# A Strassen-Winograd encoder layer: the last product of each gate/up unit moved behind the next unit's first, four early units in step, another pace for the modulation sums, another order of tile allocation

## The chip, the cores and the metric

One core of one Trainium2 chip runs one launch of the whole layer. The metric is the device time of that launch in microseconds. The trace is of one more execution, the profiled one.

## What is computed

A bidirectional encoder layer on x of 1024 tokens by 1024 features, float32. Nine vectors of 1024 (shift, scale and gate of three blocks) come from the condition c by one large matrix-vector product, and the two feed-forward blocks are SwiGLU with D_FF = 2816:

```
mod = silu(c) @ w_ada + b_ada          # 1024 x 9216, split into nine
h = modulate(rms_norm(x, g_ffn1), sh_f1, sc_f1)
x = x + 0.5 * gt_f1 * swiglu(h, w1_gu, w1_down)
h = modulate(rms_norm(x, g_mix), sh_m, sc_m)
x = x + gt_m * (concat(rms_norm(mla(h)), rms_norm(gqa(h))) @ w_out)
h = modulate(rms_norm(x, g_ffn2), sh_f2, sc_f2)
x = x + 0.5 * gt_f2 * swiglu(h, w2_gu, w2_down)
return rms_norm(x, g_final)
```

## The kernel before

Every matrix product is made of three matmuls on operands split into a high and a low part (uh and ul, B11h and B11l and so on): `split` (lines 100 to 108) casts on ScalarE (L105) and subtracts on VectorE (L106), into a ring of 9 such pairs. The gate/up product of each feed-forward block is a Winograd form of Strassen with seven products for each unit of 128 output columns of either gate or up. There are NU = 22 units. The weights A11, A12, A22 and their sums S1 to S4 are the stationary operands; the activations B11, B21, B22 and their sums T1 to T4 are the moving ones. One product of one unit is 12 matmuls of 128x512 (`prod`, L485 to L487).

For the first NE = 8 units, A11 B11 and A12 B21 are done ahead, while the T operands are still being built (`early`, `early2`, and for units 4 to 7 `early_rest`, lines 550 to 566). `run` (lines 611 to 652) then does the rest unit by unit: S2 T2, S1 T1, S3 T3, (A12 B21,) S4 B22, A22 T4. S3 T3 and A22 T4 accumulate into the same bank c. VectorE reads c after S3 T3 (`post`, L501 or L507), and only then may A22 T4 write it again. After each product `tick` (lines 200 to 205) makes two splits for units to come, and every second tick pumps one step of the stream `ada`.

That stream carries the modulation vectors that are not needed at once: seven blocks of 1024 (numbers 2, 4, 3, 5, 7, 6, 8), eight tiles each of 128x1024 (512 KB) of w_ada. For each block `ada_use` (lines 304 to 316) clears one accumulator tile acc on GpSimd (L310), loads the bias row into it (L311), and then adds each tile, times a column of silu(c), on VectorE (L313). After the eighth, TensorE sums acc over the partitions: for a gate with two matmuls by a matrix of ones (`mod_gate`, L342), for a shift or scale with eight matmuls of one column (`mod_cols`, L328). There is one acc tile, so the next block's L310 waits for those matmuls, and there are two tiles for loads (tag "ada"). What is left of the stream is done after the units, before the down projection begins:

```
    ffn.run()
    while ada.i < len(ada.specs):
        ada.pump(1)
    bg.finish()
```

The down projection (`down`) then multiplies the g tiles, written to HBM by `g_out` and loaded back, with the down weights (L729 to L731), whose quarters are summed on VectorE (L698) as they come. A scheduler sets the final order of the instructions on each engine; it may hoist an instruction whose buffers are free, and each engine runs its own list in order. SyncE issues most of the loads, in order, too.

Of the kernel before, what the change touches and what calls it, by code (L numbers as in the profile page):

```python
# [35 lines left out]
NQ0 = 4  # L36
NE = 8
# [146 lines left out]
def encoder_layer(ctx: ExitStack, tc: tile.TileContext, a: dict, out: bass.AP):  # L184
# [11 lines left out]
    st = Stream(nc, rawp, ring)  # L196
    st.raw_pools["graw"] = (lambda: t2("graw"), 2)
    bg = Background()

    def tick(n=2):  # L200
        bg.step()
        st.pump(n)
        ada_ticks[0] += 1
        if ada_ticks[0] % 2 == 0:
            ada.pump(1)


# [6 lines left out]
    def t2(name, dt=F32):  # L214
        return tmp.tile([P, 512], dt, tag="t2", name=name, bufs=6)

    def small(n, name):
        return sm.tile([P, 16], F32, tag="small", name=name, bufs=20)[:, 0:n]
# [55 lines left out]
    def use_banks(kinds):  # L274
        banks.update(kinds=kinds, n=0, pair=None)

    def ps2():
        return p2p.tile([P, 1024], F32, tag="ps2", name="ps2")

    def ps1():  # L280

        if banks["pair"] is not None:
            p = banks["pair"][:, 512:1024]
            banks["pair"] = None
            return p
        kind = banks["kinds"][banks["n"] % len(banks["kinds"])]
        banks["n"] += 1
        if kind[0] == "2":
            p = ps2()
            if kind == "2":  # L290
                banks["pair"] = p
            return p[:, 0:512]
        return (p0p if kind == "0" else p1p).tile([P, 512], F32, tag="ps1", name="ps1")
# [5 lines left out]

    ada = Stream(nc, None, None)  # L300
    ada.hold = ada.hold_step = 0
    ada_ticks = [0]

    def ada_use(blk, kt):
        def use(raw):
# [140 lines left out]
    class GateUp:  # L446
# [2 lines left out]
            self.c1, self.s, self.bank, self.g = {}, {}, {}, {}  # L449

        def alloc(self, pool, names):
            for k2 in range(2):
                for nm in names:
                    h = pool.tile([P, 2, 512], F32R, name=f"{nm}h{k2}")
                    l = pool.tile([P, 2, 512], F32R, name=f"{nm}l{k2}")
                    for e in range(2):
                        self.Bh[nm, 2 * k2 + e] = h[:, e, :]
                        self.Bl[nm, 2 * k2 + e] = l[:, e, :]
# [91 lines left out]
        def early_rest(self, builds):  # L550

            K4 = (0, 1, 2, 3)
            for u in range(NQ0, NE):
                self.bank[u] = ps1()
                self.prod(self.bank[u], u, "A11", "B11", K4, True, True)
                self.store_p1(u)
                next(builds, None)
                st.pump(2)
                bg.step()
                self.prod(self.bank[u], u, "A12", "B21", K4, False, True)  # L560
                self.early_out(u)
                next(builds, None)
                st.pump(2)
                bg.step()
            for _ in builds:
                pass

# [23 lines left out]
        def early2(self, prepare):  # L591

            K4 = (0, 1, 2, 3)
            for u in range(NQ0):
                self.bank[u] = ps1()
                self.prod(self.bank[u], u, "A11", "B11", K4, True, True)
                self.store_p1(u)
# [6 lines left out]
            for u in range(NQ0):  # L604
                self.prod(self.bank[u], u, "A12", "B21", K4, False, True)
                self.early_out(u)
# [4 lines left out]
        def run(self):  # L611
            use_banks(SIX)
            K4 = (0, 1, 2, 3)
            self.load_p1(0)
            for u in range(NU):
                early = u < NE
                self.load_p1(u + 1)
                if early and u % 2:
                    self.g["A21"] = gtp["g"]()
                    nc.sync.dma_start(self.g["A21"], ge_d[u // 2])  # L620
                if not early:
                    self.bank[u] = ps1()
                    self.prod(self.bank[u], u, "A11", "B11", K4, True, True)
                    self.keep_p1(u)
                    tick()
                c1 = self.c1.pop(u)
                b = ps1()
                self.prod(b, u, "S2", "T2", K4, True, True)
                u2 = t2("U2")
                nc.vector.tensor_tensor(u2, b, c1, op=ALU.add)  # L630
                tick()
                e = ps1()
                self.prod(e, u, "S1", "T1", K4, True, True)
                u4 = t2("U4")
                nc.vector.tensor_tensor(u4, e, u2, op=ALU.add)
                tick()
                c = ps1()
                self.prod(c, u, "S3", "T3", K4, True, True)
                self.post(u, 1, 1, c, u4)
                tick()  # L640
                if not early:
                    self.prod(self.bank[u], u, "A12", "B21", K4, False, True)
                    self.post(u, 0, 0, self.bank[u])
                    tick()
                d = ps1()
                self.prod(d, u, "S4", "B22", K4, True, True)
                self.post(u, 0, 1, d, u4)
                tick()
                self.prod(c, u, "A22", "T4", K4, False, True)
                self.post(u, 1, 0, c, u2)  # L650
                del self.bank[u]
                tick()

    def gu_specs(i):
        for u in range(NU):
# [755 lines left out]
    for s in range(NQ + LAG + 3):  # L1411
        if s < NQ:
            i, t = divmod(s, NT)
            p = scores(i, t)
            nm = small(1, "nm")
# [303 lines left out]
```

## Time and profile before

| | us |
|---|---|
| median of 3 runs | 2065.8 (2059.12 to 2625.26) |
| the profiled execution, its own time | 2058.35 |
| its span, first to last instruction | 2056.6 |
| first gate/up, early units included, in the span | 23.8 to 508.7 |
| second gate/up, early units included, in the span | 1392.3 to 1830.4 |

TensorE's granted clock was 0.984 of full speed over the span. A stretch of the trace is told by the microseconds from the start of the span. In a timeline an idle time before an instruction stands in brackets with what ended it.

### The profile page before, as it was taken

What the parts mean: (1) busy time and instruction counts of PE and PEld (TensorE: products, weight loads), DVE (VectorE), ACT (ScalarE), POOL (GpSimd) and SP (SyncE); (2) the same over time, 40 slices, a digit from 0 to 9 for tenths busy, and PEclk for the clock granted to TensorE, in tenths of its full rate; (3) what the DMA queues carried; (4) which work ended last, traced back from release to release, by engine and by line L of the source; (5) the groups of instructions that cost most, each with busy time, mean ns of one, the idle gap of its engine ahead of it and who ended that gap; (6) DMA issues with size and microseconds to landing.
All of it is one profiled execution on the core that took longest, in us unless ns stands there. A gap on an engine that the chain in (4) does not pass through costs nothing. (4 is left out here: it accounts for less than half of the span.)

```text
span 2056.6 us, 28024 instructions
## 1 busy us (share of the span) xinstructions
PE 1974.8 (96%) x10301; PEld 1678.4 (82%) x10301; DVE 1570.0 (76%) x2381; ACT 973.6 (47%) x1865; POOL 473.5 (23%) x428
## 2 busy tenths in 40 slices
PE   5889999999999999899999999998999999999998
PEld 4667888887788888788889998996788888877886
DVE  7998888974697777788798877677886666647976
ACT  6522322232344652677787777466323333324444
POOL 1643434332000023111210000005443332310011
PEclk8899999999999999999999999999999999999999
DMA  8276655544843343623253330343443332358223
GB/s 343 102 241 215 205 173 192 188 140 153 306 162 107 137 134 108 179 73 108 88 169 78 83 82 32 142 136 128 150 174 113 118 109 81 124 184 337 98 93 118
DMA packets 90550, 303.30 MB, mean 147 GB/s; under 512 B 9848, under 2 KB 22427, under 8 KB 76588
## 3 DMA queue, kind: packets, MB, share of 16 engines
q1 hardware_dynamic: 81018, 274.21, 39.5%
q0 software_dynamic: 7040, 23.07, 2.9%
q10 hardware_dynamic: 2354, 4.22, 0.5%
q8 instruction: 81, 1.33, 0.3%
q14 instruction: 57, 0.47, 0.1%
HBM read 220.98 MB, written 80.49 MB: 147 GB/s over the span
## 5 line engine op out<-in xcount | busy, mean ns | idle before, releaser
L105 ACT CAST uh<-raw 128x512 fp32r<-128x512 f32 (+1 forms) x343 | 210.3, 622 | 213.7 <-PE ps L486 134.5
L106 DVE TENSOR_TENSOR ul<-raw,uh 128x512 fp32r<-128x512 f32 (+1 forms) x343 | 255.0, 749 | 42.6 <-ACT uh L105 42.3
L105 ACT CAST uh<-S 128x512 fp32r<-128x512 f32 x198 | 121.9, 621 | 329.4 <-PE ps L486 247.4
L729 PE MATMUL ps<-uh 128*128 128x512 f32 x616 | 240.9, 393 | 5.8 <-ACT uh L105 5.8
L730 PE MATMUL ps<-ul,uh 128*128 128x512 f32 x616 | 241.5, 392 | 1.4 <-DVE ul L106 1.4
L731 PE MATMUL ps<-uh,ul 128*128 128x512 f32 x616 | 240.9, 391 | 0.0
L106 DVE TENSOR_TENSOR ul<-S,uh 128x512 fp32r<-128x512 f32 x198 | 193.7, 982 | 46.0 <-ACT uh L105 42.9
L1416 DVE TENSOR_REDUCE nm<-ps 128x1 f32<-128x1024 f32 x128 | 155.5, 1215 | 70.5 <-PE ps L223 40.8
L426 POOL TENSOR_TENSOR S<-raw 128x512 f32<-128x512 f32 x88 | 126.3, 1443 | 257.8 <-DVE ul L106 132.6
L521 POOL TENSOR_TENSOR g<-g 128x512 f32<-128x512 f32 x88 | 124.8, 1418 | 227.2 <-DVE g L508 226.3
L1434 ACT CAST ph<-ps 128x512 fp32r<-128x512 f32 x256 | 138.1, 590 | 80.0 <-PE ps L1433 79.7
L1444 DVE TENSOR_TENSOR pl<-ps,ph 128x512 fp32r<-128x512 f32 x256 | 163.9, 682 | 0.0
L1439 ACT ACTIVATE pe<-ps,nm 128x1024 f32<-128x1024 f32 x128 | 143.7, 1123 | 16.7 <-DVE nm L1416 16.5
L729 PEld LDWEIGHTS ps<-uh 128*128 128x128 f32 x616 | 116.2, 189 | 31.4 <-ACT uh L105 7.5
L730 PEld LDWEIGHTS ps<-ul,uh 128*128 128x128 f32 x616 | 116.4, 189 | 27.8 <-DVE ul L106 3.9
L731 PEld LDWEIGHTS ps<-uh,ul 128*128 128x128 f32 x616 | 116.3, 189 | 24.2
L1433 PE MATMUL ps<-ident,pe 128*128 128x128 f32 x1024 | 134.9, 273 | 0.8 <-DVE pl L1444 0.4
L1433 PEld LDWEIGHTS ps<-ident,pe 128*128 128x128 f32 x1024 | 119.7, 141 | 19.0 <-DVE pl L1444 0.6
L105 ACT CAST uh<-hT 128x512 fp32r<-128x512 f32 x96 | 59.7, 622 | 157.1 <-PE ps L730 113.5
L1382 PE MATMUL po<-ph,V 128*128 128x256 f32 x512 | 129.7, 291 | 0.0
L1383 PE MATMUL po<-pl,V 128*128 128x256 f32 x512 | 125.8, 283 | 0.0
L233 POOL TENSOR_TENSOR r<-v,neghalf 128x1 f32<-128x1 f32 x32 | 25.5, 797 | 363.9 <-DVE v L229 363.9
(280 smaller groups left out, 5180.2 us busy)
## 6 DMA issues: line engine op xcount, KB each, us to landing
raw<-in_w_gu_dram SPq DMA_DIRECT2D x52, 1024.0 KB, 4.9
ada<-in_w_ada_dram SPq DMA_DIRECT2D x56, 512.0 KB, 3.7
g_S<-g POOLq DMA_DIRECT2D x88, 256.0 KB, 2.4
g_A<-g SPq DMA_DIRECT2D x66, 256.0 KB, 3.0
hT<-in_w_down_dram SPq DMA_DIRECT2D x16, 1024.0 KB, 8.6
raw<-g_S SPq DMA_DIRECT2D x16, 1024.0 KB, 4.9
raw<-g_A SPq DMA_DIRECT2D x12, 1024.0 KB, 4.8
x<-in_x_dram SPq DMA_DIRECT2D x16, 512.0 KB, 7.3
```

What stands on the lines that cost most here:

```text
L105: nc.scalar.copy(hi[:, 0:n], ap)
L106: nc.vector.tensor_tensor(lo[:, 0:n], ap, f32(hi[:, 0:n]), op=ALU.subtract)
L426: eng.tensor_tensor(tmps[nm], get(x), get(y), op=op)
L729: nc.tensor.matmul(p, gh[:, tsl], wh, start=start, stop=False, skip_group_check=True)
L730: nc.tensor.matmul(p, gh[:, tsl], wl, start=False, stop=False, skip_group_check=True)
L731: nc.tensor.matmul(p, gl[:, tsl], wh, start=False, stop=stop, skip_group_check=True)
L1382: nc.tensor.matmul(po[:, 0:256], V, gr.ph[:, k, :], start=(k == 0), stop=False)
L1416: nc.vector.tensor_reduce(nm, p, axis=AX.X, op=ALU.max, negate=True)
L1433: nc.tensor.transpose(out=pt[:, k, :], in_=pe[:, (4 * n + k) * P:(4 * n + k + 1) * P], identity=ident)
L1434: nc.scalar.copy(gr.ph[:, 4 * n:4 * n + 4, es], pt)
L1439: nc.scalar.activation(pe, p, AF.Exp, bias=nm, accum_out=ls[:, s % 2:s % 2 + 1])
L1444: nc.vector.tensor_tensor(gr.pl[:, nsl, es], pts[n], f32(gr.ph[:, nsl, es]), op=ALU.subtract)
```

## The change

Four edits. In `run`, the last product of a unit (A22 T4) and its post go into a function that is called after the next unit's S2 T2; the last unit's is called after the loop. In `early_rest`, units 4 to 7 do all four A11 B11 products and then all four A12 B21 products. In `alloc`, the loop over names is outside, so that both tiles of B11 come first. In `tick`, the stream `ada` is pumped by a rate in eighths; the rate is a list that holds 0, and no other line of the file writes it, so the condition `0 > 0` is never true and the 56 steps are all reached by the loop after `run`.

```
-        if ada_ticks[0] % 2 == 0:
+        if ada_ticks[0] * ada_rate[0] // 8 > (ada_ticks[0] - 1) * ada_rate[0] // 8:
             ada.pump(1)
...
-    ada_ticks = [0]
+    ada_ticks, ada_rate = [0], [0]
...
-            for k2 in range(2):
-                for nm in names:
+            for nm in names:
+                for k2 in range(2):
...
-            for u in range(NQ0, NE):
+            for u0 in range(NQ0, NE, 4):
+                us = range(u0, u0 + 4)
+                for u in us:
                     self.bank[u] = ps1()
                     self.prod(self.bank[u], u, "A11", "B11", K4, True, True)
                     self.store_p1(u)
...
+                for u in us:
                     self.prod(self.bank[u], u, "A12", "B21", K4, False, True)
                     self.early_out(u)
...
                 nc.vector.tensor_tensor(u2, b, c1, op=ALU.add)
                 tick()
+                if tail:
+                    tail.pop()()
                 e = ps1()
...
-                self.prod(c, u, "A22", "T4", K4, False, True)
-                self.post(u, 1, 0, c, u2)
-                del self.bank[u]
-                tick()
+                def last(u=u, c=c, u2=u2):
+                    self.prod(c, u, "A22", "T4", K4, False, True)
+                    self.post(u, 1, 0, c, u2)
+                    del self.bank[u]
+                    tick()
+                tail.append(last)
+            tail.pop()()
```

The order on TensorE before, where the first gate/up ends (T4 is the last unit's last product) and the down projection begins (its first row is L729):

```order
L485 MATMUL ps_4063<-T4h_576,uh 128x512
L486 MATMUL ps_4063<-T4l_577,uh 128x512
L487 MATMUL ps_4063<-T4h_576,ul 128x512
L729 MATMUL ps_4176<-uh 128x512
L729 MATMUL ps_4177<-uh 128x512
L729 MATMUL ps_4179<-uh 128x512
```

The same place on TensorE in the change (L328 and L342 are the matmuls of the modulation vectors, L740 the first of the down projection):

```order
L487 MATMUL ps_3804<-T4h_576,ul 128x512
L342 MATMUL ps_3908<-acc,ones 128x512
L342 MATMUL ps_3913<-acc,ones 128x512
L328 MATMUL ps_3945<-ones,acc 128x1 x8
L328 MATMUL ps_3982<-ones,acc 128x1 x8
L342 MATMUL ps_4019<-acc,ones 128x512
L342 MATMUL ps_4024<-acc,ones 128x512
L328 MATMUL ps_4056<-ones,acc 128x1 x8
L328 MATMUL ps_4093<-ones,acc 128x1 x8
L342 MATMUL ps_4126<-acc,ones 128x512
L342 MATMUL ps_4131<-acc,ones 128x512
L740 MATMUL ps_4176<-uh 128x512
```

All seven blocks' matmuls, which stood between the units before, now stand in a row ahead of the first down product.

VectorE in the change from the last post of gate/up (the first row) on; the list goes on with the rest of the 48 sums, and the next split for down stands behind the last of them:

```order
L507 TENSOR_TENSOR g<-ps_3804,U_3772 128x512
L106 TENSOR_TENSOR ul<-hT,uh 128x512
L508 TENSOR_TENSOR g<-g,s 128x512
L106 TENSOR_TENSOR ul<-raw,uh 128x512
L106 TENSOR_TENSOR ul<-hT,uh 128x512
L106 TENSOR_TENSOR ul<-raw,uh 128x512
L106 TENSOR_TENSOR ul<-hT,uh 128x512
L106 TENSOR_TENSOR ul<-raw,uh 128x512
L106 TENSOR_TENSOR ul<-hT,uh 128x512
L106 TENSOR_TENSOR ul<-raw,uh 128x512
L313 SCALAR_TENSOR_TENSOR acc<-ada,cact,acc 128x1024 x8
L333 SCALAR_TENSOR_TENSOR modA_111<-ps_3945,cols 128x8
```

The first block's eight sums stay early in gate/up, because its acc and its loads find free buffers; the other 48 moved to the end, and 11 of the sums of L698 (L709 in the change) stand among them.

TensorE before, in the third unit of the first gate/up, from S4 B22 to A22 T4:

```order
L487 MATMUL ps_1210<-B22h_568,ul 128x512
L485 MATMUL ps_1210<-B22h_568,uh 128x512
L486 MATMUL ps_1210<-B22l_569,uh 128x512
L487 MATMUL ps_1210<-B22h_568,ul 128x512
L485 MATMUL ps_1188<-T4h_566,uh 128x512
L486 MATMUL ps_1188<-T4l_567,uh 128x512
```

The same place in the change:

```order
L487 MATMUL ps_1185<-B22h_560,ul 128x512
L485 MATMUL ps_1213<-T2h_566,uh 128x512
L486 MATMUL ps_1213<-T2l_567,uh 128x512
L487 MATMUL ps_1213<-T2h_566,ul 128x512
L485 MATMUL ps_1213<-T2h_566,uh 128x512
L486 MATMUL ps_1213<-T2l_567,uh 128x512
L487 MATMUL ps_1213<-T2h_566,ul 128x512
L485 MATMUL ps_1213<-T2h_568,uh 128x512
L486 MATMUL ps_1213<-T2l_569,uh 128x512
L487 MATMUL ps_1213<-T2h_568,ul 128x512
L485 MATMUL ps_1213<-T2h_568,uh 128x512
L486 MATMUL ps_1213<-T2l_569,uh 128x512
```

One whole product of the next unit now stands between S4 B22 and A22 T4 (12 matmuls, of which the last is not shown).

## Rows read from the trace of the kernel before

**Rows 1.** The page, part 1: busy us, share, instructions of each engine.

```profile
PE 1974.8 (96%) x10301; PEld 1678.4 (82%) x10301; DVE 1570.0 (76%) x2381; ACT 973.6 (47%) x1865; POOL 473.5 (23%) x428
```

**Rows 2.** Stretches: us, busy (count) by engine, PE clock, DMA share, GB/s.

```profile
110.00:200.00 90.00, 79.83 (x332) 63.55 (x331) 82.68 (x93) 23.59 (x39) 34.16 (x29) 0.96 0.67 226
300.00:400.00 100.00, 99.75 (x453) 82.11 (x452) 84.94 (x101) 28.47 (x50) 36.39 (x34) 1.00 0.56 187
1400.00:1500.00 100.00, 88.16 (x382) 71.20 (x381) 79.99 (x87) 46.93 (x90) 52.09 (x36) 0.97 0.39 138
1500.00:1600.00 100.00, 100.00 (x443) 82.80 (x442) 72.29 (x94) 30.06 (x49) 39.87 (x36) 1.00 0.39 137
```

**Rows 3.** PE's waits, 0 to 110 us: total, times, longest.

```profile
PE ps L485 <- POOL acc L310: 3.5, 1, 3.5
```

**Rows 4.** PE's waits, 110 to 200 us.

```profile
PE ps L485 <- DVE s L501: 9.4, 3, 5.0
```

**Rows 5.** Timeline of PE, 140 to 155 us: start, duration, operation [idle before].

```profile
148.06 0.76 PE L485 MATMUL ps<-T4h,uh 128*128 128x512 f32 x1 [5.00 <-DVE s L501]
...
154.24 0.39 PE L485 MATMUL ps<-T2h,uh 128*128 128x512 f32 x1
```

**Rows 6.** PE's waits, 1380 to 1500 us.

```profile
PE ps L485 <- ACT c L493: 9.3, 2, 7.6
```

**Rows 7.** Tile acc: count, duration ns min/median/max, first and last start.

```profile
L328 PE MATMUL ps<-ones,acc x64: 164/250/250, 211.2 to 397.0; 128*128 128x1 f32 x64
L313 DVE SCALAR_TENSOR_TENSOR acc<-ada,cact,acc x56: 1269/1280/5112, 113.8 to 425.9; 128x1024 f32<-128x1024 f32 x56
...
L342 PE MATMUL ps<-acc,ones x12: 591/592/593, 161.7 to 442.8; 128*128 128x512 f32 x12
L310 POOL MEMSET acc<- x7: 947/955/976, 96.1 to 402.5; 128x1024 f32 x7
```

**Rows 8.** Timeline of PE: matmuls of modulation vectors, three places.

```profile
18.91 1.87 PE L910 MATMUL modp<-ones,acc 128*128 128x1 f32 x8 [1.77 <-DVE acc L783]
...
161.75 1.88 PE L342 MATMUL ps<-acc,ones 128*128 128x512 f32 x4
163.06 0.79 PE L485 MATMUL ps<-B22h,uh 128*128 128x512 f32 x1
...
211.20 1.84 PE L328 MATMUL ps<-ones,acc 128*128 128x1 f32 x16
```

**Rows 9.** Timelines, SyncE's queue and VectorE, 402 to 428 us: last block.

```profile
403.53 0.25 SPq L311 DMA_DIRECT2D acc<-in_b_ada_dram  x1
406.41 0.33 SPq L95 DMA_DIRECT2D ada<-in_w_ada_dram  x1
...
405.09 1.29 DVE L313 SCALAR_TENSOR_TENSOR acc<-ada,cact,acc 128x1024 f32<-128x1024 f32 x1 [0.73 <-issue]
...
410.06 1.29 DVE L313 SCALAR_TENSOR_TENSOR acc<-ada,cact,acc 128x1024 f32<-128x1024 f32 x1
...
425.87 1.28 DVE L313 SCALAR_TENSOR_TENSOR acc<-ada,cact,acc 128x1024 f32<-128x1024 f32 x1
```

**Rows 10.** The page, part 6: DMA issues, KB each, us to landing.

```profile
raw<-in_w_gu_dram SPq DMA_DIRECT2D x52, 1024.0 KB, 4.9
ada<-in_w_ada_dram SPq DMA_DIRECT2D x56, 512.0 KB, 3.7
```

**Rows 11.** Timelines of PE and of DVE where gate/up 1 ends.

```profile
509.04 1.20 PE L729 MATMUL ps<-uh 128*128 128x512 f32 x4 [0.30 <-ACT uh L105]
...
508.83 0.69 DVE L507 TENSOR_TENSOR g<-ps,U 128x512 f32<-128x512 f32 x1 [1.30 <-PE ps L487]
...
517.57 0.68 DVE L106 TENSOR_TENSOR ul<-raw,uh 128x512 fp32r<-128x512 f32 x1
```

**Rows 12.** Line 698: the sums of weight quarters for down.

```profile
L698 DVE TENSOR_TENSOR hT<-hT x48: 679/685/692, 564.9 to 1937.9; 128x512 f32<-128x512 f32 x48
```

**Rows 13.** PE's waits, 200 to 560 us.

```profile
PE ps L729 <- ACT uh L105: 2.2, 2, 1.9
```

More of the change, by code (lines that the diff above doesn't have):

```diff
@@ L552, in early_rest @@
             K4 = (0, 1, 2, 3)
-            for u in range(NQ0, NE):
[L554 to L564, printed above, removed]
+            for u0 in range(NQ0, NE, 4):
+                us = range(u0, u0 + 4)
+                for u in us:
+                    self.bank[u] = ps1()
+                    self.prod(self.bank[u], u, "A11", "B11", K4, True, True)
+                    self.store_p1(u)
+                    next(builds, None)
+                    st.pump(2)
+                    bg.step()
+                for u in us:
+                    self.prod(self.bank[u], u, "A12", "B21", K4, False, True)
+                    self.early_out(u)
+                    next(builds, None)
+                    st.pump(2)
+                    bg.step()
             for _ in builds:
@@ L613, in run @@
             K4 = (0, 1, 2, 3)
+            tail = []
             self.load_p1(0)
```

## Prediction

> **What bounds the kernel now.** I read the page first: TensorE is busy 96% of the span, VectorE 76% [rows 1]. Then the stretches of 50 to 100 us. In the middle of both gate/up phases TensorE has no gap (99.75 and 100.00 of 100 us) and starts 443 matmuls in 100 us, 0.226 us each, so one product of 12 takes 2.71 us there. Two stretches have gaps: 110 to 200 us, with 79.83 of 90 us busy at a clock of 0.96, and 1400 to 1500 us, with 88.16 [rows 2]. The list of waits names them: in the first TensorE waits 9.4 us in three places for L501, VectorE's read of bank c ahead of A22 T4 [rows 4]; in the second 9.3 us for L493, ScalarE's copy of an early unit's bank [rows 6]. The modulation sums cost TensorE nothing but their own few matmuls, since VectorE does them beside the products. So the change can win only in those two stretches, and it can lose wherever TensorE is made to wait.
>
> **The part that decides: the sums.** The rate holds 0 and nothing sets it, so no tick pumps the stream. The order shows the result: 8 sums stay early, 48 stand behind the last post of gate/up 1, and all the matmuls of the seven vectors stand on TensorE ahead of the first down product. TensorE cannot pass them, and the splits for down that are made before them fill the ring of 9 pairs. So the whole chain of sums is idle time of TensorE. I count it from 508.83 us, where VectorE's last post starts and the last product has ended [rows 11].
>
> Start: before the first of the 48 sums VectorE has the post and eight splits. The same eight splits took until 517.57 + 0.68 us in the trace [rows 11], 9.4 us after 508.83. The matmuls of the block that was summed early, L310 and the bias row lie beside this.
>
> One block of eight sums: the first two tiles are loaded already, each later tile needs a free one of two buffers. A sum takes 1.28 us [rows 7]. In the trace a load is issued 0.03 us after the sum that frees its buffer (405.09 + 1.29, then 406.41), and the sum that uses it starts 3.65 us later, at 410.06 [rows 9]; the page has 3.7 us [rows 10]. So two tiles take 1.28 + 0.03 + 3.7 = 5.01 us, and a block takes three such rounds and two sums: 15.0 + 2.6 = 17.6 us. Six blocks: 105.6 us. VectorE alone would need 6 x 8 x 1.28 = 61.4 us; the two buffers make the rest.
>
> Between two blocks: TensorE sums acc, GpSimd clears it (0.955 us) [rows 7], the bias row is loaded (1.56 us from the issue at 403.53 to the sum at 405.09) [rows 9], with some 0.15 us of signals. TensorE will have idled, and after idle time it runs at the lower of its clocks, 1.2 GHz: behind the wait of 5.00 us the 15 matmul starts up to 154.24 us took 6.2 us for 3.4 [rows 5], and 8 one-column matmuls at the start of the kernel took 1.87 us where 16 took 1.84 us in the busy stretch [rows 8]. So a shift or scale takes 3.7 us and a gate 2.6 us (twice the 1.31 us from 161.75 to 163.06) [rows 8]. Four transitions behind shifts and scales: 4 x 6.4 = 25.6 us; one behind a gate, with its copy and two stores in SyncE's queue ahead of the bias: 5.7 us; the last gate's matmuls: 2.6 us.
>
> The 11 sums of weight quarters that stand among them take 0.685 us each [rows 12], 7.5 us if none fell into the waits for loads; 4 us is my value, about half. Loads of down weights pass in the same queue between the pairs; at 1.2 us for each further 512 KB (4.9 less 3.7) [rows 10] a round of 5 us has room for one of 1 MB and the pair, so I add nothing.
>
> Sum: 9.4 + 105.6 + 25.6 + 5.7 + 2.6 + 4 = 152.9 us, less 0.2 us from 508.83 to 509.04 that stood there before: **+152.7 us**. Behind it down starts at the lower clock: 6.2 less 3.4 [rows 5], **+2.8 us**.
>
> The bounds: if the loads were ready always, a block would be 10.2 us and the stall 108. If each block took as long as the last one in the trace, 425.87 + 1.28 less 405.09 = 22.1 us, with other work and loads between [rows 9], it would be 180.
>
> The Trainium skill's page "DMA: Bandwidth & Descriptors", section "Anatomy of one DMA", puts the fixed part of a transfer at about 2.0 us. The trace's two sizes give 3.7 less 1.2 = 2.5 us. An estimate by the page: loads of 3.2 us, 18 rounds each 0.5 us shorter, a total 9 us lower than mine. The rows decide here, since they are these very loads.
>
> **What comes back in the first gate/up.** The matmuls of the vectors leave a TensorE that has no gaps: 64 rows at L328 are four vectors at 1.84 us, 12 at L342 three gates at 1.31 us [rows 7, 8]: **-11.3 us**. They are in the chain above. The moved A22 T4 gives VectorE 2.71 us more to read bank c. Of the waits of 9.4 us the one of 5.00 keeps 2.3 and the other two, 4.4 us together, go almost whole; with no sums on VectorE after the first block and a shorter slow stretch behind I take **-10 us**, between 0 (VectorE is just as late at the next bank) and -13 (all waits and the 2.8 us of slow clock). What is queued behind the moved product: the next unit's S1 T1, which needs nothing from it. The order on TensorE had started the next S2 T2 early here and there already, so nothing new must be ready.
>
> **Early units in step, and the allocation.** In the first feed-forward block the longest wait of the early part, 3.5 us, is for room for the T tiles, not for an early unit [rows 3]; the scheduler had interleaved the units in the old loop already. I take 0, with 3.5 us to either side. In the second, TensorE waits 7.6 us of the 9.3 for one copy [rows 6], and the copy keeps its place on ScalarE behind the casts of the T operands. TensorE has six more matmuls to do first (1.4 us), and the second wait, 9.3 less 7.6 = 1.7 us, is covered by whole products: **-3 us**, between 0 and -9.3. The order of names in the allocation moves no instruction; nothing. In the second gate/up proper there is no wait to win [rows 2].
>
> **At the start of down** TensorE waited 2.2 us for casts whose data came late [rows 13]. With 150 us to load it this is gone: **-2 us**.
>
> **Total:** 152.7 + 2.8 - 11.3 - 10 - 3 - 2 = +129 us on the profiled execution's 2058.35 us: 2187.6, so **2188 us**. That execution stands 7 us under the median of 2065.8 and 1 us under the lowest of the three; I keep its scale. A measurement tells about 2% from no change, some 41 us; three times that is forecast.
>
> **The rivals.**
> Loads hidden: if the pairs of loads kept ahead of VectorE, six blocks would be 7.4 us shorter each: 2188 - 44 = 2144 us. For it: only that the queue has room. Against it: two buffers, and the load is longer than two sums. 4%.
> Loads in each other's way: every block as long as the last one of the trace, 22.1 us: 2188 + 27 = 2215 us. For it: the down weights load through the same queue meanwhile. Against it: half the blocks run after these are in, and VectorE has no other work. 8%.
> Nothing comes back in the waits: without the -10, -3 and -2 it is 2203 us. For it: VectorE is 82.68 of 90 us busy from 110 to 200 us [rows 2], where the 8 early sums stay. 5%.
> Not slower: down's products run while the sums go on, because TensorE is fed from the ring and the vectors are needed much later. Then the stall is nothing, the slow clock too, the matmuls are only moved, and 2058 - 10 - 3 = 2045 us is left. It decides from the point at which TensorE idles under some 26 us at the end of gate/up, what the other terms give back. Against it: the rows on TensorE ahead of L740. 3%.
>
> **How the numbers follow.** My case has 80%. Its ends: fast clock in the transitions (-9), sums of quarters hidden (-4), loads shorter by the estimate's 9 us or waits that all go (-10), about 2155 us; blocks longer by 4 us, nearly the second rival's, 2212 us. The range 2152 to 2212 us takes in the third rival and leaves the first and most of the second outside. Slower by over 2%: 0.96; within 2%: 0.03; faster: 0.01.
>
> **What would show it.** After: TensorE idle but for the vectors' matmuls for about 150 us from some 490 us on, the clock low there; six groups of eight sums at L313, each 17 to 18 us long, in pairs 5 us apart; 6 us between groups, with L310 released by TensorE; the waits for L501 from 110 to 200 us under 5 us. Wrong would be: sums closer than 2 us throughout, down matmuls between the vectors', gaps of 10 us between blocks, or a gate/up phase that ends later than before.

## The result, and the profile after

The changed kernel takes 2194.6 us (median of 4 runs, 2193.35 to 2197.02); before it was 2062.9 us (median of 4). The ratio is 1.0646, with a 95% interval of 1.0621 to 1.0672; one run before, of 2625.26 us, is left out of it as slow. The forecast was 2188 us within 2152 to 2212. The profiled execution took 2194.53 us, with a span of 2192.8 us, 136.2 us longer than that of the profiled execution before.

The page of the changed kernel, TensorE's and its clock's rows of part 2 behind that of part 1, which answers to [rows 1]; in part 2 each digit is a slice of 54.8 us:

```profile
PE 1976.8 (90%) x10301; PEld 1683.7 (77%) x10301; DVE 1532.5 (70%) x2381; ACT 975.9 (45%) x1865; POOL 465.5 (21%) x428
...
PE   6889999981129999999999999999799999999998
...
PEclk7999999995559999999999999999999999999999
```

TensorE is busy as long as before (1976.8 for 1974.8 us) in a longer span. The missing time is one hole of three slices, and in them the clock stands near the lower of its two levels. The list of TensorE's waits says who made the hole. First the stretch from 470 to 720 us, then 110 to 480 us, to be held against [rows 4], and the two longest from 1500 to 1650 us, against [rows 6] (total, times, longest):

```profile
PE ps L328 <- DVE acc L313: 97.5, 4, 30.4
PE ps L342 <- DVE acc L313: 45.7, 2, 23.7
```

```profile
PE ps L485 <- DVE s L501: 5.0, 2, 4.1
PE ps L485 <- DVE g L507: 2.3, 1, 2.3
```

```profile
PE ps L485 <- ACT c L493: 8.3, 2, 6.2
PE ps L485 <- ACT es L502: 3.0, 1, 3.0
```

Six waits, one for each block that was left, cost 143.2 us (97.5 + 45.7). TensorE's timeline through the hole (start, duration, operation, idle before):

```profile
485.70 1.88 PE L342 MATMUL ps<-acc,ones 128*128 128x512 f32 x4
518.01 3.58 PE L328 MATMUL ps<-ones,acc 128*128 128x1 f32 x16 [30.43 <-DVE acc L313]
545.78 3.57 PE L328 MATMUL ps<-ones,acc 128*128 128x1 f32 x16 [24.20 <-DVE acc L313]
573.02 3.78 PE L342 MATMUL ps<-acc,ones 128*128 128x512 f32 x4 [23.66 <-DVE acc L313]
...
648.72 3.62 PE L342 MATMUL ps<-acc,ones 128*128 128x512 f32 x4 [22.01 <-DVE acc L313]
651.49 1.09 PE L740 MATMUL ps<-uh 128*128 128x512 f32 x1
```

The first vector was summed early and costs nothing. The other six stand in a row ahead of L740, the first down matmul, as the order had shown. VectorE's last post starts at 485.96 us, so the stall, counted as in the forecast from there to the first down matmul, is 651.49 - 485.96 = 165.5 us. VectorE's timeline shows what fills it, first in the first of the six blocks, then in the fifth:

```profile
485.96 0.69 DVE L507 TENSOR_TENSOR g<-ps,U 128x512 f32<-128x512 f32 x1 [1.30 <-PE ps L487]
...
495.21 2.59 DVE L313 SCALAR_TENSOR_TENSOR acc<-ada,cact,acc 128x1024 f32<-128x1024 f32 x2
500.52 1.28 DVE L313 SCALAR_TENSOR_TENSOR acc<-ada,cact,acc 128x1024 f32<-128x1024 f32 x1 [2.72 <-DMA ada<-in_w_ada_dram]
...
507.23 1.28 DVE L313 SCALAR_TENSOR_TENSOR acc<-ada,cact,acc 128x1024 f32<-128x1024 f32 x1 [2.85 <-DMA ada<-in_w_ada_dram]
...
513.57 1.28 DVE L313 SCALAR_TENSOR_TENSOR acc<-ada,cact,acc 128x1024 f32<-128x1024 f32 x1 [2.64 <-DMA ada<-in_w_ada_dram]
516.67 1.28 DVE L313 SCALAR_TENSOR_TENSOR acc<-ada,cact,acc 128x1024 f32<-128x1024 f32 x1 [1.82 <-DMA ada<-in_w_ada_dram]
...
604.09 2.60 DVE L313 SCALAR_TENSOR_TENSOR acc<-ada,cact,acc 128x1024 f32<-128x1024 f32 x2 [2.46 <-DMA acc<-in_b_ada_dram]
609.02 1.28 DVE L313 SCALAR_TENSOR_TENSOR acc<-ada,cact,acc 128x1024 f32<-128x1024 f32 x1 [2.33 <-DMA ada<-in_w_ada_dram]
611.38 1.28 DVE L313 SCALAR_TENSOR_TENSOR acc<-ada,cact,acc 128x1024 f32<-128x1024 f32 x1 [1.08 <-DMA ada<-in_w_ada_dram]
613.99 1.28 DVE L313 SCALAR_TENSOR_TENSOR acc<-ada,cact,acc 128x1024 f32<-128x1024 f32 x1 [1.32 <-DMA ada<-in_w_ada_dram]
...
618.98 1.29 DVE L313 SCALAR_TENSOR_TENSOR acc<-ada,cact,acc 128x1024 f32<-128x1024 f32 x1 [1.26 <-DMA ada<-in_w_ada_dram]
621.78 1.28 DVE L313 SCALAR_TENSOR_TENSOR acc<-ada,cact,acc 128x1024 f32<-128x1024 f32 x1 [1.52 <-DMA ada<-in_w_ada_dram]
```

In these two blocks only the first pair finds its tiles loaded; each later sum is released by a load. In the fifth block the pairs start 4.93, 4.97 and 4.99 us apart, in the first 5.31, 6.71 and 6.34. SyncE's queue in the first block shows what differs (x2 are the two loads of a pair):

```profile
496.51 1.65 SPq L95 DMA_DIRECT2D ada<-in_w_ada_dram  x2
498.20 0.43 SPq L86 DMA_DIRECT2D hT<-in_w_down_dram  x1
501.84 2.90 SPq L95 DMA_DIRECT2D ada<-in_w_ada_dram  x2
504.79 0.42 SPq L86 DMA_DIRECT2D hT<-in_w_down_dram  x1
```

Behind each of these pairs stands a load of down weights, of 1 MB (behind the third pair of the block it is one of 0.75 MB, behind the last none). In the fifth block the queue has eight loads of ada from 605.40 us on and nothing between them. The page's part 6 has the median time from issue to landing, to be held against [rows 10]:

```profile
ada<-in_w_ada_dram SPq DMA_DIRECT2D x56, 512.0 KB, 4.5
```

And four stretches: the middle of gate/up (against [rows 2]), the hole, and in it the first and the fifth block (length, then busy time and count of PE, PEld, DVE, ACT, POOL, then clock, DMA share, GB/s):

```profile
300.00:400.00 100.00, 100.00 (x442) 82.80 (x442) 58.49 (x84) 32.64 (x54) 35.52 (x33) 1.00 0.29 100
490.00:650.00 160.00, 19.29 (x70) 15.91 (x71) 74.05 (x68) 2.07 (x4) 9.19 (x11) 0.52 0.67 220
495.00:518.00 23.00, 0.00 (x0) 0.00 (x0) 10.47 (x9) 0.00 (x0) 0.56 (x1) 0.50 0.89 330
604.00:623.00 19.00, 0.00 (x0) 0.00 (x0) 10.21 (x8) 0.00 (x0) 0.00 (x0) 0.50 0.65 190
```

In the hole no engine is busy half of the time, and the DMA engines are so 0.67 of it. That mean hides two stages: in the first block, with the down weights behind the pairs, the DMA engines are busy 0.89 of the time and move 330 GB/s; in the fifth, where the sums' loads are alone, 0.65 and 190 GB/s, and there the latency of the loads sets the pace. In the middle of gate/up TensorE was full before and is full now, with a third of VectorE's work gone (58.49 for 84.94 us). What was taken off VectorE there had not kept TensorE waiting.

### The profile page after: what moved, and what is told of

The parts are those of the page before. It is cut to its first block, busy times and chain, and to the rows that moved or that the text cites. A ratio compares the mean times of both kernels' runs of the same rounds, so it can differ in the third digit from the quotient of the medians.

```text
span 2192.8 us, 28026 instructions
## 1 busy us (share of the span) xinstructions
PE 1976.8 (90%) x10301; PEld 1683.7 (77%) x10301; DVE 1532.5 (70%) x2381; ACT 975.9 (45%) x1865; POOL 465.5 (21%) x428
## 5 line engine op out<-in xcount | busy, mean ns | idle before, releaser
L740 PE MATMUL ps<-uh 128*128 128x512 f32 x616 | 240.5, 391 | 2.8 <-ACT uh L105 2.8
L106 DVE TENSOR_TENSOR ul<-S,uh 128x512 fp32r<-128x512 f32 x198 | 158.0, 803 | 55.3 <-ACT uh L105 55.3
L1445 ACT CAST ph<-ps 128x512 fp32r<-128x512 f32 x256 | 138.1, 590 | 79.7 <-PE ps L1444 79.6
L426 POOL TENSOR_TENSOR S<-raw 128x512 f32<-128x512 f32 x88 | 118.8, 1360 | 203.1 <-DMA raw<-in_w_gu_dram 99.3
L740 PEld LDWEIGHTS ps<-uh 128*128 128x128 f32 x616 | 115.7, 188 | 28.0 <-ACT uh L105 3.6
L313 DVE SCALAR_TENSOR_TENSOR acc<-ada,cact,acc 128x1024 f32<-128x1024 f32 x56 | 74.3, 1328 | 66.3 <-DMA ada<-in_w_ada_dram 52.1
```

What stands on the lines that cost most here:

```text
L106: nc.vector.tensor_tensor(lo[:, 0:n], ap, f32(hi[:, 0:n]), op=ALU.subtract)
L740: nc.tensor.matmul(p, gh[:, tsl], wh, start=start, stop=False, skip_group_check=True)
L1445: nc.scalar.copy(gr.ph[:, 4 * n:4 * n + 4, es], pt)
```

## The experiments

Three questions were open: whether the rate alone makes the whole loss, what paces a block, and what the other three edits are worth.

**Which edit costs.** The kernel before, with nothing changed but that no tick pumps the stream:

```
-        if ada_ticks[0] % 2 == 0:
+        if ada_ticks[0] < 0:
             ada.pump(1)
```

> The kernel before, with the stream of modulation sums pumped at no tick, and nothing else changed. Theory A, the pace of the sums alone makes the loss: 48 sums stand behind gate/up 1 as in the changed kernel, the stall is 160 to 170 us, and since the product A22 T4 is not moved the waits for L501 are at most a few us more: 2190 to 2206 us. Rival B, a good part of the loss comes from the three other edits (the moved product, the units in step, the allocation): under 2180 us.

Measured: 2196.8 us, ratio 1.0675 (1.0648 to 1.0701). TensorE's waits from 110 to 720 us in it:

```profile
PE ps L328 <- DVE acc L313: 97.5, 4, 29.1
PE ps L342 <- DVE acc L313: 44.1, 2, 23.0
PE ps L485 <- DVE s L501: 7.0, 2, 5.5
```

The same six waits, and a time 2 us above the changed kernel's: the rate makes the whole loss, with none of the other edits there. The opposite try is the changed kernel at the old pace, four eighths, from the start:

```
-    ada_ticks, ada_rate = [0], [0]
+    ada_ticks, ada_rate = [0], [4]
```

> The changed kernel with the rate at 4 eighths from the start, which is the pace of the kernel before: the three other edits alone. Theory A: the stall is gone, and the three edits are worth 0 to 12 us, nearly all of it from the waits for L501 between 110 and 200 us: 2048 to 2060 us. Rival B: they cost time by themselves, over 2070 us.

Measured: 2052.2 us, ratio 0.9965 (0.9951 to 0.9979). The hole is gone, and what is left beats the kernel before, by about 7 us.

**The sums from the ninth unit on**: the changed kernel with a rate of six eighths set when the units that are not early begin.

```
             for u in range(NU):
                 early = u < NE
+                if u == NE:
+                    ada_rate[0] = 6
```

> The changed kernel with one line more: the rate is set to 6 eighths at the ninth unit of gate/up 1. Theory A: all 56 sums but the first eight run beside the late units, where VectorE was 66 to 85 of 100 us busy; no stall, and the early units are free of them: 2040 to 2056 us. Rival C, 48 sums in 14 units crowd VectorE (48 x 1.28 = 61 us in some 230): TensorE waits for splits or for bank reads there, 2062 to 2090 us.

Measured: 2058.0 us, ratio 0.9994 (0.9983 to 1.0004): no gain over the kernel before, and 6 us behind the old pace. TensorE's waits from 110 to 520 us, first with the sums from the ninth unit on, then with the old pace:

```profile
PE ps L485 <- DVE s L501: 4.9, 2, 4.1
PE ps L328 <- DVE acc L313: 2.4, 1, 2.4
PE ps L485 <- DVE g L507: 2.3, 1, 2.3
PE ps L328 <- ACT c L493: 1.3, 1, 1.3
```

```profile
PE ps L485 <- DVE s L501: 4.6, 2, 4.0
PE ps L485 <- DVE g L507: 3.3, 2, 1.6
PE ps L485 <- ACT s L502: 2.0, 1, 2.0
```

The waits for the posts are 7.2 us with the stream held back beside the first units and 9.9 with it. Against these 2.7 us stand two waits of 3.7 us in all at the vectors' matmuls, where the old pace has none; in the 60 us around each (280 to 340 and 380 to 440 us) the clock is 0.97, where it is 1.00 at the old pace. Over these 120 us that is 3.6 us, and with the 1.0 us of waits it comes near to the whole difference from the first T2 product to the first down matmul (406.7 us, and 401.8 at the old pace). So the closer pace gives back more than the late start wins. The time lies between the bands of the two theories: a gain from the late start is not there, and the closer pace costs less than was feared.

**What paces a block.** Three kernels do all seven blocks after the first gate/up, from a pool of their own that opens when gate/up's tiles are gone. The first has six tiles for loads, the second the same and two accumulators, the third two tiles for loads:

```
...
+    es_ = ExitStack()
+    ep = es_.enter_context(tc.tile_pool(name="ep", bufs=1))
+    t4pool["p"] = (ep, 1)
+    ada.raw_pools["raw"] = (lambda: ep.tile([P, D], F32, tag="ada", name="ada", bufs=6), 6)
...
+    while ada.i < len(ada.specs):
+        ada.pump(1)
```

Six tiles:

> The changed kernel with the loads of the sums in a pool of six tiles in place of two, which has room only after gate/up: all seven blocks then stand behind it. Theory A, the two buffers pace the chain: a block of eight sums takes 10.3 to 12 us in place of 18 to 23, the stall is 9 + 7 x 11 + 6 x 6.4 + 3 = 127 us with one block more, and the time 2150 to 2165 us. Rival D, the queue's bandwidth, shared with the down weights, paces it: blocks stay at 18 us or more, the stall is 175 us or more with one block more, and the time 2200 us or more.

Measured: 2171.3 us (one execution). VectorE's first two blocks:

```profile
501.62 10.53 DVE L313 SCALAR_TENSOR_TENSOR acc<-ada,cact,acc 128x1024 f32<-128x1024 f32 x8 [13.81 <-DMA acc<-in_b_ada_dram]
518.56 10.53 DVE L313 SCALAR_TENSOR_TENSOR acc<-ada,cact,acc 128x1024 f32<-128x1024 f32 x8 [6.41 <-DMA acc<-in_b_ada_dram]
```

Eight sums without a gap, 10.53 us, are VectorE's own time (8 x 1.28 = 10.2), so the rival, a queue whose bandwidth holds the blocks at 18 us, falls. The time is 6 us above what was expected: the first sum starts 23.1 us behind the last post, where 9 had been reckoned. SyncE issues the first loads of ada only at 491.42 us, the bias row behind them, and the first sum waits for that row.

Two accumulators (`t4pool["p"] = (ep, 2)`):

> All seven blocks behind gate/up 1 with six tiles for loads, as in the earlier run, and two accumulators in place of one. Theory A, between blocks VectorE waits 6 us for TensorE's matmuls, the clearing and the bias row because there is one accumulator: these six gaps go nearly whole, and the time is 2135 to 2148 us against 2171. Rival, the loads (56 of 512 KB) hold the pace once the gaps are gone: gaps of 3 us or more between the groups, 2150 to 2165 us.

Measured: 2145.7 us (one execution), 25.6 us less. VectorE's first blocks in it:

```profile
498.15 9.21 DVE L313 SCALAR_TENSOR_TENSOR acc<-ada,cact,acc 128x1024 f32<-128x1024 f32 x7 [13.85 <-DMA acc<-in_b_ada_dram]
508.14 8.96 DVE L313 SCALAR_TENSOR_TENSOR acc<-ada,cact,acc 128x1024 f32<-128x1024 f32 x7 [0.78 <-DMA ada<-in_w_ada_dram]
```

The first block's eighth sum waits 0.78 us for its load, and the second block's first six follow it with no gap. So the 6.4 us between these two blocks came from the single accumulator. But the six gaps did not go nearly whole, as was expected: three later groups still waited 5 to 6 us, bias rows among the causes. From the first sum to the end of the last VectorE is idle 26 us, where with one accumulator the six transitions made 38: 12 us are saved, and that is all that the second accumulator shows. Of the other 13 us, 3.5 lie in the earlier start (498.15 for 501.62 us) and between 6 and 7 in the 11 sums of weight quarters, which stand among the blocks with one accumulator and behind them with two; the rest lies behind the stall. That the time fell into the band of the first theory was luck. Even so this stands 86 us above the kernel before.

Two tiles in the same place (`bufs=2`):

> The counterpart of the run with six tiles for loads: all seven blocks behind gate/up 1, in a pool of their own that has room only then, but with two tiles. Theory A, the two buffers make a block 18 us or more: 7 blocks x (19.5 less 10.5) = 63 us over the run with six tiles, 2225 to 2245 us. Rival, the late start or the shared queue made the difference between the runs so far: within 25 us of the run with six tiles.

Measured: 2218.8 us (one execution), 6 us below the expected band and 47.5 above six tiles. The start of its first block on VectorE:

```profile
494.81 2.60 DVE L313 SCALAR_TENSOR_TENSOR acc<-ada,cact,acc 128x1024 f32<-128x1024 f32 x2 [8.13 <-DMA ada<-in_w_ada_dram]
501.05 1.28 DVE L313 SCALAR_TENSOR_TENSOR acc<-ada,cact,acc 128x1024 f32<-128x1024 f32 x1 [3.63 <-DMA ada<-in_w_ada_dram]
```

The seven blocks took 21.1, 20.0, 18.6, 18.7, 18.6, 20.1 and 18.6 us, 135.6 in all, where six tiles took 79.7. The number of tiles alone makes 8 us in each block, and 56 us in seven; most of the way from there to 47.5 is the earlier start of the first sum (494.81 for 501.62 us). The rival, that the late start or the shared queue made the difference, falls.

**Who stands in the way of the loads.** The changed kernel, with the down weights' quarters issued from ScalarE's queue in place of SyncE's:

```
-                    self.nc.sync.dma_start(src[0](), src[1])
+                    self.nc.scalar.dma_start(src[0](), src[1])
```

> The changed kernel with the loads of the down weights' quarters issued by ScalarE's queue, where they stand in a row early in the stall and no longer between the pairs of loads for the sums. Theory A, a load of 1 MB ahead of a pair makes the first three blocks longer (22.7, 21.4 and 20.8 us against 18.3, 19.0 and 19.4 for the others): the first block takes 23 to 32 us, the second and third 18 to 19.5 us and what their weight sums add, under 2 us; the stall is 155 to 166 us, the time 2184 to 2196 us. Rival, the first blocks are long for another reason: the second and third stay at 20.5 to 21.5 us, and the time stays at 2194 us or rises.

Measured: 2202.7 us, ratio 1.0692 (1.0674 to 1.0710). VectorE's timeline, the first block and the start of the second:

```profile
496.76 3.71 DVE L313 SCALAR_TENSOR_TENSOR acc<-ada,cact,acc 128x1024 f32<-128x1024 f32 x2 [2.75 <-DMA acc<-in_b_ada_dram]
507.87 1.28 DVE L313 SCALAR_TENSOR_TENSOR acc<-ada,cact,acc 128x1024 f32<-128x1024 f32 x1 [7.40 <-DMA ada<-in_w_ada_dram]
...
517.43 1.28 DVE L313 SCALAR_TENSOR_TENSOR acc<-ada,cact,acc 128x1024 f32<-128x1024 f32 x1 [5.05 <-DMA ada<-in_w_ada_dram]
...
525.54 1.28 DVE L313 SCALAR_TENSOR_TENSOR acc<-ada,cact,acc 128x1024 f32<-128x1024 f32 x1
...
533.59 2.60 DVE L313 SCALAR_TENSOR_TENSOR acc<-ada,cact,acc 128x1024 f32<-128x1024 f32 x2
```

Now the down weights come together: from 495 to 527 us the DMA engines are busy 0.96 of the time and move 382 GB/s. The first block takes 30.1 us, and the second and third, 21.4 and 20.8 us in the changed kernel, take 18.5 and 19.05, as long as the blocks behind them (18.8 to 19.0). So it is the down weights' traffic that makes the early blocks longer, and another queue for it changes only which block pays: 124.4 us for the six, where it was 121.7. The mechanism was foreseen and the time was not: it came out above the band. The stall in the trace is 169.8 us (655.91 - 486.14), 4.3 us longer than in the changed kernel; the rest of the 8 us is not explained. The Trainium skill's page "DMA: Bandwidth & Descriptors", section "Issuing engines are not separate DMA queues", says that transfers of all issuing engines run on the same 16 DMA engines and interleave, so that spreading them saves only issue time; the rounds of 11.1 and 9.6 us in the first block agree.

**What the other edits are worth**, each at the old pace. The moved A22 T4 alone; then with the units in step but the old allocation; then with the allocation but the old early loop. The hunks are those of the diff ahead of the prediction, taken singly into the kernel before (for the first: `tail` and `last` in `run`; for the second `us = range(u0, u0 + 4)` in `early_rest` too; for the third `for nm in names` outside in `alloc`), and `[0], [4]` for the rate.

> The kernel before with the moved product A22 T4 alone, at the old pace of the sums. Theory A, read from the run with all three edits (10 us less between the first T2 product and down 1, 3 us less in gate/up 2, but 2 and 4 us more in the two early parts): the moved product brings 13 to 15 us and the units in step take back 6, so this alone is the fastest, 2043 to 2049 us. Rival: the early parts' loss belongs to the moved product or is noise, 2050 to 2056 us.

> The moved product and the units in step, with the old order of allocation, at the old pace. Theory A, the allocation moves nothing: 2050 to 2055 us, as with all three. Rival, the allocation makes the loss in the early parts: 2043 to 2049 us.

> The moved product and the new order of allocation, with the old loop over the early units, at the old pace. Theory A, the units in step make the loss in the early parts: 2043 to 2049 us, the early part before the second block's first T2 product 51 to 52 us. Rival, the allocation makes it: 2050 to 2056 us and 55 to 56 us.

| at the old pace | us | ratio, 95% | start to start of the second early part | from there to the second down |
|---|---|---|---|---|
| moved product alone | 2053.7 | 0.9957 to 0.9985 | 51.7 | 386.8 |
| moved product and step | 2053.6 | 0.9956 to 0.9983 | 55.6 | 383.7 |
| moved product and allocation | 2051.5 | 0.9944 to 0.9971 | 51.7 | 387.0 |
| all three | 2052.2 | 0.9951 to 0.9979 | 55.7 | 383.5 |

(The last two columns are of one trace each: from the first B11 product of the second feed-forward block to its first T2 product, and from there to its first down matmul. Before they were 51.7 and 386.7 us.) The four can't be told apart by their intervals. The moved product makes the whole gain, 6 to 8 us, less than the 13 to 15 us that I had expected of it; the step and the allocation are worth nothing that shows. The times of the first and the third run ended in the bands of their rivals: the step moves 4 us from one part of the trace to the other, as the table shows, but takes no time from the whole.

## Why the prediction was right, and where it was off

The forecast rested on one step, that the rate of 0 puts 48 sums and their matmuls ahead of the first down matmul and that TensorE cannot pass them. That step held in every part: the order, the six groups, one buffer's latency for each pair where no other load was in the way, the clear of acc behind TensorE's read. The rival "not slower" fell with the six waits, "loads hidden" with the waits for ada: 32 of them, 52.1 us in all. "Loads in each other's way" was half right: it is what the three first blocks show. The terms one by one, on the two profiled executions:

| term | forecast | measured |
|---|---|---|
| start: post and splits to the first sum | 9.4 | 495.21 - 485.96 = 9.25 |
| six blocks, with the weight quarters' sums | 105.6 + 4 | 121.7 |
| five transitions | 25.6 + 5.7 | 6.4, 6.4, 6.5, 6.3, 6.2: 31.8 |
| last gate's matmuls | 2.6 | 2.9 |
| stall in all, from the last post | 152.9 | 165.5 |
| gate/up's end comes earlier | 11.3 + 10 = 21.3 | 508.83 - 485.96 = 22.9 |

**The term that was mis-sized is the block.** It was 17.6 us in the forecast and 22.7, 21.4, 20.8, 18.3, 19.0 and 19.4 in the trace, 12 us more in all than the 105.6 + 4. Two steps failed: the first is worth some 4 us of the 12, the second some 8.

The first is the sentence on the down weights, "so I add nothing". Nine loads of down weights, of 0.75 or 1 MB, are issued from 495 to 560 us, one behind most pairs. The forecast gave a round of 5 us room for 1 MB and the pair, some 2 MB: that would be 420 GB/s. The first block's stretch moved 330 GB/s with the DMA engines busy 0.89 of the time, and its rounds took 5.3 to 6.7 us. The move to ScalarE's queue shows it from the other side. The first three blocks are 8.3 us longer together than the last three, and the forecast had only the 4 us of the weight quarters' sums for that.

The second is the round itself. The rounds of a block that is free of other loads were right (4.93 to 4.99 us for 5.01), but they count the first tile alone. SyncE issues the second tile's load at 606.72 us, 1.3 us behind the first, and its sum starts at 611.38, 4.7 us later, where the first took 3.6. The second tile's sums stay behind by that and more (its later loads took 3.7 and 4.0 us), so the last sum starts 2.80 us behind the one ahead of it and not 1.28. That is 1.5 us in this block; the last three blocks lie 0.7 to 1.8 us over 17.6, and six such blocks would be 7.8 us over 105.6.

The prediction's estimate by the Trainium skill, loads of 3.2 us and a total 9 us lower, lay on the wrong side of the rows here. The Trainium skill's page "DMA: Bandwidth & Descriptors" gives that fixed part, in its section "Anatomy of one DMA — SWDGE (gpsimd) path", for transfers issued from GpSimd. These loads are issued from SyncE: the trace of the kernel before had 3.7 us, and of the fourth block's loads here the quickest took 3.46 us to its sum (593.04 to 596.50).

**The slow clock behind the stall** was put at 2.8 us. After the hole the first down matmul took 1.09 us and the next ones start 0.23 us apart, so it cost at most 0.7 us.

**What came back in gate/up** came out in size (22.9 for 21.3), but it hangs on the moved product less than I thought. The kernel before with only the rate changed has no moved product, and its way from the first T2 product to the first vectors' matmul behind gate/up is 388.4 us, where the kernel before has 411.7 to its first down matmul: 23.3 us less, of which the matmuls of the vectors are 11.3 (at the durations before) and the waits 9; the remaining 3 go with a clock of 0.97 for 0.94 from 97 to 200 us. All waits of TensorE in this stretch add to 16.3 us before, 7.3 without the sums, 7.3 without them and with the moved product, and, in the run with all three edits at the old pace, 9.9 with the moved product and the sums. So either edit takes 6 to 9 us of waits away, and the moved product adds 2 us to what the missing sums bring (386.0 us for 388.4). The wait of 5.00 us for L501 [rows 5], of which 2.3 were to be left, kept 4.1.

**The units in step** were to win 3 us. The waits for early units only changed places: the longest for L493 went from 7.6 to 6.2 us, the 1.4 us that were forecast, but the other one for L493 went from 1.7 to 2.0 and was not covered, and that for L502 went from 1.9 to 3.0; with the small ones they add to 12.7 us before and 12.5 after. In the traces with the step the first T2 product comes 4 us later and most of this is made up behind it (table above), a net of nothing. The step of the prediction that failed is that the six matmuls ahead would shorten one wait while no other grew.

**The rest.** From the first down matmul to the second block's first B11 product the changed kernel was 5.0 us shorter (2 us forecast), but the traces of the kernels above spread from 878 to 885 us in this place, so no part of that is counted as explained. All in all the errors are +12.6 us for the stall and some 6 us the other way, and the median came out 6.6 us above the forecast. That it came out so near is in part luck, since the errors ran against each other.

## What to carry to other kernels

Work that a scheduler runs beside the bottleneck for nothing is paid in full when it is moved to a place where nothing else runs, and there it can cost the latency of its buffers and not its busy time: here 61 us of sums cost 165 us of stall with two buffers, one accumulator and a competing stream. When such a chain must stand alone, count the rounds first (load latency over the number of tiles, and the accumulator's clear between groups), and the bytes of all the loads in a round against the rate that the trace reaches. Here six tiles gave 8 us back in each block and a second accumulator about 12 us in seven, but the place beside the products gave back all of it. Before taking work off an engine, look in the stretch itself whether anybody waits for that engine: in the middle of gate/up nobody did.

## What the runs showed of the hardware that I had not expected

A load of 512 KB that is issued 1.3 us behind another takes 4.6 to 4.7 us until its sum starts, where the one ahead takes 3.6 (first pairs of the fourth, fifth and sixth block), although the DMA engines are busy only 0.65 of the fifth block. With 0.75 or 1 MB of other loads behind a pair a round of two goes from 5.0 to 5.3 to 6.7 us; there the DMA engines are busy 0.89 of the time.

The clock at the first down matmul differs between kernels whose TensorE did the same before it, a wait of 21 to 22 us and one gate's four matmuls. The kernel before with only the rate changed:

```profile
648.81 3.75 PE L342 MATMUL ps<-acc,ones 128*128 128x512 f32 x4 [21.14 <-DVE acc L313]
651.57 1.42 PE L729 MATMUL ps<-uh 128*128 128x512 f32 x1
...
653.63 0.63 PE L729 MATMUL ps<-uh 128*128 128x512 f32 x1
```

In the changed kernel the gate's four took 3.62 us and the first down matmul 1.09, with the upper clock right behind it (0.23 us from start to start); here they took 3.75 and 1.42, and the next matmuls still ran at 0.63 us (0.43 from start to start, the lower clock). What decides it is open; the difference up to the seventh down matmul is about 1 us.
